# Log-sum-exp over rows: splitting the rows 111 and 17 per partition instead of 112 and 16

## Chip, cores and metric

The kernel runs on one core of one Trainium2 chip. The metric is device time in microseconds, the median of several executions. Lower is better.

## What is computed

The input `x` has shape 32 x 512 x 1024 in float32 (64 MB). For each of its 16,384 rows of 1024 values the kernel returns the logarithm of the sum of exponentials:

```python
def reference(x):
    max_x = np.max(x, axis=-1, keepdims=True)
    return (max_x.squeeze(-1) + np.log(np.sum(np.exp(x - max_x), axis=-1))).astype(np.float32)
```

The inputs are drawn from a normal distribution, so the kernel sums plain exponentials without subtracting the maximum, checks that no sum is out of bounds, and only if one is repeats everything with the maximum taken off.

## The kernel before

There are 128 rows for each of the 128 partitions. They come from two regions of the input. In the first, partition p holds `W = 112` rows that follow one another in memory; in the second it holds `B = 16` rows that do so (`x_rows` and `x_rest`, lines 81 and 82). The output is written in the same two regions, with one store each (`out_rows`, line 329, and `out_rest`, line 343).

The rows travel through a ring in SBUF with room for 48 rows per partition. SyncE issues all loads on one queue, in order (line 157). Before each load it waits until the reductions that read that part of the ring are over; `users` keeps the list.

The first region comes in the nine loads of `LOADS`, each with its size in rows and with what is done to it. ScalarE takes the exponential of each group in place (line 236). A group marked R is then summed by VectorE over all 1024 columns (line 251). A group marked F is first folded by GpSimd, which adds the second half of each row to the first (line 244); VectorE then sums 512 columns per row (line 199, in `reduce_folded`). `F2+2` means two folds of two rows each.

The second region comes in nine "late" loads, whose sizes get smaller. The order is: from column `HEAD` = 528 of the region to `start`; from row `MID` to 608 columns (`BACK`) before the end; the five `PIECES`, which fill the space from `start` to row `MID`; the last 608 columns; the first 528 columns. `start` is `MID * d - sum(PIECES)`, with `d` = 1024. ScalarE takes the exponential of each piece (line 294). As soon as a row of the region is complete, VectorE sums it by adding its two halves with an accumulator (`halves`, line 208). Rows cut by `HEAD` and `BACK` are summed in parts, and the parts of the first pass are joined to the last two pieces as logarithms (line 322), so that the last two exponentials (lines 287 and 279) sum them on ScalarE.

In the middle of this ScalarE takes the logarithm of the first region's sums (line 314), and VectorE checks the columns that are ready (`check_early`, lines 166 and 171). TensorE adds up the later checks in one PSUM cell (line 186). At the end come a last check on VectorE (lines 334 and 351), the last logarithms on ScalarE (lines 339 and 341), the second store, and the test of the check (line 358), on which the branch depends.

The order on each engine is the order of the code, and each engine waits on semaphores that the others count up.

Of the kernel before, what the change touches and what calls it, by code (L numbers as in the profile page):

```python
# [13 lines left out]
CEILING = 27.0  # L14
STEEP = 2.0**48
RING = 48
B = 16
GAP = 32
AHEAD = 1
FIRST = 512  # L20
# [1 line left out]

LOADS = [
    (16, "R16"), (16, "R16"), (16, "R16"), (16, "F9 R7"), (13.5, "F6 R7"), (12.5, "R7 F6"),
    (9, "R5 F4"), (7, "F4 R3"), (6, "F2+2 R2"),
]

HEAD, BACK, MID = 528, 608, 12  # L30
PIECES = [2656, 2000, 1456, 1088, 800]


# [23 lines left out]
def kernel(  # L57
# [21 lines left out]
    H = d // 2  # L79
    W = NC - B  # L80
    x_rows = x_flat[0 : P * W].rearrange("(p c) d -> p (c d)", p=P)
# [15 lines left out]
    start = MID * d - sum(PIECES)  # L97
    late = [(HEAD, start), (MID * d, B * d - BACK)]
    for size in PIECES:
        late.append((start, start + size))  # L100
        start += size
    late += [(B * d - BACK, B * d), (0, HEAD)]
    assert start == MID * d and sum(e - s for s, e in late) == B * d
    LATE = W + late[0][1] // d
# [114 lines left out]
    for i, (size, ops) in enumerate(loads):  # L219
# [37 lines left out]
        assert here == end  # L257
    assert c == W and here == p and p + GAP + B * d <= RING * d

    gap = p + (B - MID) * d  # L260

# [212 lines left out]
```

## Time and profile before

| | |
|---|---|
| median of 3 runs | 161.6 us (161.47 to 161.63) |
| the profiled execution | 161.53 us |
| its span, first to last instruction | 160.2 us |
| granted clock | 1.000 |
| VectorE busy | 114.2 us (71% of the span) |
| ScalarE busy | 114.5 us (71%) |
| GpSimd busy | 37.3 us (23%) |
| load queue's share of the 16 DMA engines | 97.9% |
| read from HBM | 67.11 MB |

Times in the profile count from the first instruction of the span. "ACT" is ScalarE, "DVE" is VectorE, "POOL" is GpSimd, "SP" is SyncE and "SPq" its queue, where DMAs are issued. A line of the timeline gives start, duration, engine, line and operation, and in brackets how long the engine was idle before and what ended it. In the groups by line and shape, the number behind the bar is the busy time in us, then the mean of one in ns, then the idle time before. A DMA issue is shown with its size and the time from issue to landing.

### The profile page before, as it was taken

The numbers are of one execution on the slowest core, as the hardware profiler recorded it, in microseconds if no ns is written. First come the engines' busy times: TensorE is split into PE (matmuls) and PEld (weight loads), VectorE is DVE, ScalarE is ACT, GpSimd is POOL, SyncE is SP. The second block draws the span as 40 slices with busy tenths as digits, with TensorE's granted clock in tenths as the row PEclk, the third lists the DMA queues.
The fourth block names the chain that finished last, engine by engine and source line by source line (L and its number), as shares of the span: only waits on it lengthen the run. The fifth ranks groups of instructions, "written<-read, shape, count | busy, mean of one in ns | idle before, by whom it ended". The sixth has DMA issues, their size and how long they took to land.

```text
span 160.2 us, 236 instructions
## 1 busy us (share of the span) xinstructions
PE 2.3 (1%) x32; PEld 1.2 (1%) x32; DVE 114.2 (71%) x60; ACT 114.5 (71%) x31; POOL 37.3 (23%) x11
## 2 busy tenths in 40 slices
PE   0000000000000000000000000000000000000023
PEld 0000000000000000000000000000000000000011
DVE  0000000019999499994999859959999999999996
ACT  3000059980799709995099949992999989799996
POOL 0000000000000000000000994690004969765000
DMA  9996996996996996996999999999989999999993
GB/s 319 507 491 269 507 524 262 524 524 262 524 524 262 524 507 278 524 491 295 483 442 442 442 425 409 409 409 481 414 387 445 458 409 393 425 433 425 414 405 111
DMA packets 3025, 67.18 MB, mean 419 GB/s; under 512 B 592, under 2 KB 592, under 8 KB 1488
## 3 DMA queue, kind: packets, MB, share of 16 engines
q1 hardware_dynamic: 3024, 67.18, 97.9%
q14 instruction: 1, 0.01, 0.0%
HBM read 67.11 MB, written 0.07 MB: 419 GB/s over the span
## 4 chain that ended last, share of the span: by engine, by line
DMA 51%; ACT 27%; DVE 20%; issue 0%; PE 0%
DMA ring<-in_x_dram 51%; ACT ring L236 19%; DVE sumexp L251 16%; ACT ring L294 7%; DVE sumexp L199 2%; DVE ring L208 2%; DVE over L351 0%; PE count L356 0%; ACT res L314 0%; DVE clamped L334 0%; DVE fine L358 0%; ACT ring L322 0%
## 5 line engine op out<-in xcount | busy, mean ns | idle before, releaser
L236 ACT ACTIVATE ring<-ring 128x16384 f32<-128x16384 f32 (+9 forms) x15 | 97.9, 6568 | 42.3 <-DMA ring<-in_x_dram 42.3
L251 DVE TENSOR_REDUCE sumexp<-ring 128x16 f32<-128x16384 f32 (+4 forms) x9 | 85.6, 9515 | 42.4 <-ACT ring L236 42.4
L244 POOL TENSOR_TENSOR ring<-ring 128x3072 f32<-128x3072 f32 (+3 forms) x7 | 37.1, 5313 | 108.8 <-ACT ring L236 108.8
L199 DVE TENSOR_REDUCE sumexp<-ring 128x6 f32<-128x3072 f32 (+3 forms) x7 | 18.4, 2657 | 0.0
L294 ACT ACTIVATE ring<-ring 128x3760 f32<-128x3760 f32 (+6 forms) x7 | 13.9, 2009 | 0.0
L208 DVE SCALAR_TENSOR_TENSOR ring<-ring 128x512 f32<-128x512 f32 (+2 forms) x16 | 9.5, 650 | 0.1
L142 ACT ACT_TABLE_LOAD x1 | 1.3, 1283 | 1.9 <-PEq L66 1.9
L176 PE MATMUL count<-far,bad 128*1 128x1 f32 x2 | 0.2, 164 | 152.9 <-DVE clamped L171 152.9
L186 PE MATMUL count<-sumexp,ones 128*1 128x1 f32 x24 | 1.9, 164 | 3.5 <-DVE ring L208 3.5
L143 DVE MEMSET ones<- 128x1 f32 x1 | 0.1, 59 | 2.0 <-PEq L66 2.0
L208 DVE DVE_READ_ACCUMULATOR ring<-ring 128x1 f32 x16 | 1.3, 82 | 0.0
L176 PEld LDWEIGHTS count<-far,bad 128*1 128x1 f32 x2 | 0.1, 80 | 152.9 <-DVE clamped L171 152.9
L186 PEld LDWEIGHTS count<-sumexp,ones 128*1 128x1 f32 x24 | 0.9, 81 | 4.4 <-DVE ring L208 4.4
L287 ACT ACTIVATE ring<-ring 128x610 f32<-128x610 f32 x1 | 0.7, 696 | 0.0
L279 ACT ACTIVATE last_exp<-ring 128x530 f32<-128x530 f32 x1 | 0.6, 595 | 0.0
L351 DVE SCALAR_TENSOR_TENSOR over<-ring 128x264 f32<-128x264 f32 x1 | 0.4, 427 | 0.0
L358 DVE TENSOR_SCALAR fine<-count 1x1 int32<-1x1 f32 x1 | 0.1, 146 | 0.3 <-PE count L356 0.3
L171 DVE SCALAR_TENSOR_TENSOR clamped<-clamped,sumexp 128x117 f32<-128x117 f32 x1 | 0.3, 281 | 0.0
L314 ACT ACTIVATE res<-sumexp 128x112 f32<-128x112 f32 x1 | 0.3, 280 | 0.0
L166 DVE TENSOR_SCALAR clamped<-sumexp 128x117 f32<-128x117 f32 x1 | 0.2, 224 | 0.0
L339 ACT ACTIVATE res<-sumexp 128x15 f32<-128x15 f32 x1 | 0.2, 203 | 0.0
L334 DVE SCALAR_TENSOR_TENSOR clamped<-sumexp 128x12 f32<-128x12 f32 x1 | 0.2, 170 | 0.0
(20 smaller groups left out, 2.3 us busy)
## 6 DMA issues: line engine op xcount, KB each, us to landing
ring<-in_x_dram SPq DMA_DIRECT2D x1, 7936.0 KB, 21.3
ring<-in_x_dram SPq DMA_DIRECT2D x1, 6912.0 KB, 23.9
ring<-in_x_dram SPq DMA_DIRECT2D x1, 6400.0 KB, 19.7
ring<-in_x_dram SPq DMA_DIRECT2D x1, 4608.0 KB, 15.9
ring<-in_x_dram SPq DMA_DIRECT2D x1, 3584.0 KB, 24.0
ring<-in_x_dram SPq DMA_DIRECT2D x1, 3072.0 KB, 19.1
ring<-in_x_dram SPq DMA_DIRECT2D x1, 1880.0 KB, 16.0
ring<-in_x_dram SPq DMA_DIRECT2D x1, 1744.0 KB, 19.8
```

The lines of the kernel that those rows point to most:

```text
L142: nc.scalar.preload_act_table_set("natural_log_exp_and_others")
L176: pe.did(nc.tensor.matmul(count, lhsT=bad[:, 0:1], rhs=far, start=True, stop=False))
L186: pe.did(nc.tensor.matmul(count, lhsT=ones, rhs=sumexp[:, c : c + 1], start=False, stop=False))
L199: at = dve.did(nc.vector.reduce_sum(out=sumexp[:, c0 : c0 + s0], in_=halves, axis=AX.X))
L208: return dve.did(nc.vector.scalar_tensor_tensor(out=v[:, 0:n], in0=v[:, 0:n], scalar=1.0, in1=v[:, n : 2 * n], op0=ALU.mult, op1=ALU.add, ...
L236: at = act.did(nc.scalar.activation(out=v, in_=v, func=AF.Exp))
L244: at = pool.did(nc.gpsimd.tensor_tensor(out=lo, in0=lo, in1=rows[:, r : r + m, H:d], op=ALU.add))
L251: at = dve.did(nc.vector.reduce_sum(out=sumexp[:, c : c + s], in_=rows, axis=AX.X))
L279: head_sum = act.did(nc.scalar.activation(out=last_exp[:, 0 : e - s + 2], in_=ring[:, at0 - 2 : at1], func=AF.Exp, accum_out=last_sum,))
L287: back_sum = act.did(nc.scalar.activation(out=v, in_=v, func=AF.Exp, accum_out=sumexp[:, NC - 1 : NC]))
L294: at = act.did(nc.scalar.activation(out=v, in_=v, func=AF.Exp))
L351: dve.did(nc.vector.scalar_tensor_tensor(out=over, in0=ring[:, at0 : at0 + half], scalar=CEILING, in1=ring[:, at0 + half : at1], op0=ALU.m ...
```

## The change

The second region gets 17 rows per partition instead of 16, and so the first region 111 instead of 112. The ninth load has 5 rows instead of 6, of which 3 instead of 4 are folded (two and one). `MID` moves from 12 to 13, so that the five pieces and the other three late loads keep their sizes. The first late load goes from column 528 to column 5312 of the region and has 4784 columns instead of 3760; one more of the region's rows is complete with it. The rows of one partition lie 111 rows (444 KB) and 17 rows (68 KB) behind those of the partition before it in memory, instead of 448 and 64 KB. The two stores write 444 and 68 bytes per partition instead of 448 and 64.

```diff
-B = 16
+B = 17
...
 LOADS = [
     (16, "R16"), (16, "R16"), (16, "R16"), (16, "F9 R7"), (13.5, "F6 R7"), (12.5, "R7 F6"),
-    (9, "R5 F4"), (7, "F4 R3"), (6, "F2+2 R2"),
+    (9, "R5 F4"), (7, "F4 R3"), (5, "F2+1 R2"),
 ]
...
-HEAD, BACK, MID = 528, 608, 12
+HEAD, BACK, MID = 528, 608, 13
 PIECES = [2656, 2000, 1456, 1088, 800]
```

## The prediction

> **What bounds the kernel now.** I read the page first, then the chain of waits in order of time, the DMA issues, and last the timeline of the final 45 us engine by engine.
>
> ```profile
> span 160.2 us, 236 instructions
> q1 hardware_dynamic: 3024, 67.18, 97.9%
> DMA 51%; ACT 27%; DVE 20%; issue 0%; PE 0%
> ```
>
> The load queue is busy for 97.9% of the 16 DMA engines' time. The chain gives DMA only 51%, because it follows one releaser at each step. So the load stream sets the pace, and the question is what happens behind its last pieces.
>
> ```profile
> 118.89 19.10 DMA ring<-in_x_dram
> 138.01 5.42 ACT ring L236 x2
> 143.43 6.32 ACT ring L294 x2
> ...
> 154.20 1.31 ACT ring L294
> 155.54 2.55 DVE ring L208 x8
> ```
>
> The chain leaves DMA at 138.0, when the ninth load (six rows) lands. From there it runs over ScalarE's exponentials, and over four row sums on VectorE at the end. Whether ScalarE is really the limit is told by the landings, which come from the issue times (SPq rows) and the times to landing:
>
> ```profile
> 126.42 0.33 SPq L157 DMA_DIRECT2D ring<-in_x_dram  x1
> 126.79 1.38 SPq L157 DMA_DIRECT2D ring<-in_x_dram  x3
> ring<-in_x_dram SPq DMA_DIRECT2D x1, 1880.0 KB, 16.0
> ring<-in_x_dram SPq DMA_DIRECT2D x1, 1744.0 KB, 19.8
> ring<-in_x_dram SPq DMA_DIRECT2D x1, 1000.0 KB, 24.5
> 138.01 5.42 ACT L236 ACTIVATE ring<-ring 128x4096 f32<-128x4096 f32 x2 [1.03 <-DMA ring<-in_x_dram]
> 143.33 6.41 ACT L294 ACTIVATE ring<-ring 128x3760 f32<-128x3760 f32 x2
> 146.64 3.11 ACT L294 ACTIVATE ring<-ring 128x3488 f32<-128x3488 f32 x1
> 149.84 4.27 ACT L294 ACTIVATE ring<-ring 128x2656 f32<-128x2656 f32 x2
> L294 ACT ACTIVATE ring<-ring 128x2000 f32<-128x2000 f32 x1 | 1.9, 1870 | 0.0
> ```
>
> The first late load (1880 KB) is issued at 126.42 and lands 16.0 later, at 142.4. ScalarE takes it at 143.33, 0.9 us late, because it is still busy with the ninth load. The second (1744 KB) lands at 126.79 + 19.8 = 146.6, and ScalarE takes it at 146.64, that is, at its landing. The fourth (1000 KB) is the third of the three issues from 126.79; with about 0.45 us between issues it goes out near 127.7 and lands at 152.2. The last row's two exponentials end at 149.84 + 4.27 = 154.11, so the second (2000 columns, 1.87 us) starts at 152.2, again at its landing. After that ScalarE has no gap up to the last store. So the end is the landing of the fourth late load plus a fixed piece of ScalarE's work. What lies before 152.2 counts only if it moves a landing, or makes ScalarE miss one.
>
> **The change part by part.** The loads. The ninth load falls from 6 to 5 rows and the first late one grows from 3760 to 4784 columns, which is the same 1024. The two lie next to each other in the queue, so the first late load and all that follow land where they did. The number of transfers is unchanged. The ninth load itself lands earlier by 1024 columns:
>
> ```profile
> 41.09 13.86 ACT L236 ACTIVATE ring<-ring 128x16384 f32<-128x16384 f32 x1 [5.49 <-DMA ring<-in_x_dram]
> 60.45 13.86 ACT L236 ACTIVATE ring<-ring 128x16384 f32<-128x16384 f32 x1 [5.50 <-DMA ring<-in_x_dram]
> ```
>
> Two loads of 16 rows are 19.36 us apart, so a row takes 1.21 us and the ninth load lands at 138.0 - 1.2 = 136.8. SP's waits are the same: the ninth load overwrites rows that the same reduction frees, the first late load waits for the same two reductions, and the later pieces fall on the same places of the ring, because the start moves down a row and the piece offset moves up one. The late load is issued at 126.4 and the queue is occupied with the ninth until 136.8, so 10 us of cover are left for that issue.
>
> ScalarE, with these rows:
>
> ```profile
> 130.71 6.27 ACT L236 ACTIVATE ring<-ring 128x4096 f32<-128x4096 f32 x2 [0.54 <-DMA ring<-in_x_dram]
> L236 ACT ACTIVATE ring<-ring 128x4096 f32<-128x4096 f32 x3 | 10.8, 3612 | 1.6 <-DMA ring<-in_x_dram 1.6
> L236 ACT ACTIVATE ring<-ring 128x5120 f32<-128x5120 f32 x1 | 4.5, 4471 | 0.0
> L236 ACT ACTIVATE ring<-ring 128x3072 f32<-128x3072 f32 x1 | 2.7, 2748 | 0.0
> L236 ACT ACTIVATE ring<-ring 128x2048 f32<-128x2048 f32 x1 | 1.9, 1893 | 0.0
> ```
>
> The eighth load's exponentials end at 130.71 + 6.27 = 136.98, so the ninth load now finds ScalarE busy for 0.2 us instead of idle for 1.03. Its two exponentials have 3072 and 2048 columns, 2.75 + 1.89 less an overlap of 0.09 (3.61 + 1.89 against the 5.42 in the timeline), so they end at 136.9 + 4.55 = 141.5. ScalarE then waits for the landing at 142.4. The exponential of 4784 columns costs, between the rows of 4096 and 5120 (0.84 ns a column), 3612 + 688 x 0.84 = 4190 ns, and the next can start 4.10 after it: 142.45 + 4.10 = 146.55. The second late load lands at 146.6. The longer piece just fits, with 0.05 to 0.1 to spare, where before it started 0.9 late and was 0.85 shorter. Another 0.1 is lost harmlessly between 149.84 and the landing at 152.2. ScalarE's term is 0.
>
> VectorE and GpSimd:
>
> ```profile
> 140.82 2.28 DVE L199 TENSOR_REDUCE sumexp<-ring 128x4 f32<-128x2048 f32 x1
> 143.46 2.29 DVE L251 TENSOR_REDUCE sumexp<-ring 128x2 f32<-128x2048 f32 x1 [0.37 <-ACT ring L236]
> 145.66 2.34 DVE L199 TENSOR_REDUCE sumexp<-ring 128x2 f32<-128x1024 f32 x2
> 147.92 0.68 DVE L208 SCALAR_TENSOR_TENSOR ring<-ring 128x512 f32<-128x512 f32 x1
> 154.14 0.69 DVE L208 SCALAR_TENSOR_TENSOR ring<-ring 128x512 f32<-128x512 f32 x1
> 155.54 0.69 DVE L208 SCALAR_TENSOR_TENSOR ring<-ring 128x512 f32<-128x512 f32 x1
> L199 DVE TENSOR_REDUCE sumexp<-ring 128x4 f32<-128x2048 f32 x2 | 4.6, 2276 | 0.0
> L199 DVE TENSOR_REDUCE sumexp<-ring 128x2 f32<-128x1024 f32 x2 | 2.3, 1210 | 0.0
> L208 DVE SCALAR_TENSOR_TENSOR ring<-ring 128x512 f32<-128x512 f32 x14 | 8.9, 687 | 0.1
> L244 POOL TENSOR_TENSOR ring<-ring 128x1024 f32<-128x1024 f32 x2 | 4.7, 2359 | 2.4 <-ACT ring L236 2.4
> ```
>
> One folded row leaves the ninth load. The second folded reduction shrinks from 1024 to 512 columns; by the two L199 rows that is 1210 - 533 = 0.68 us, 0.53 saved. GpSimd's second addition halves to some 1.2 us, and its pair, starting at 139.7, ends at 143.3, well before VectorE asks for it. One more row sum (L208) comes with the first late load: 0.61 us, the pitch at which they follow each other (0.69 with its tail overlapped). The reduction of the last two rows no longer waits 0.37 for ScalarE: it starts at 143.1 when VectorE is free. So the row sums can start at 143.1 + 2.2 + 1.1 + 0.7 = 147.1 or 147.2 instead of 147.92, and after five instead of four VectorE stands 0.1 earlier than before. That is worth nothing, because at 154.14 and 155.54 VectorE waits for exponentials that end at 154.11 and 155.51, and the last four sums follow the second of these as before. If the savings failed, the extra 0.61 would meet a slack of about 0.11 at 154.14 and 0.17 at 155.54 (each start less the end of the row sum before it, at a pitch of 0.61). VectorE's term is 0.
>
> The stores. The logarithms and checks change by one column; their term is 0. Each partition's result piece becomes 444 and 68 bytes instead of 448 and 64.
>
> ```profile
> 158.76 0.34 SPq L343 DMA_DIRECT2D out_dram<-res  x1
> out_dram<-res SPq DMA_DIRECT2D x1, 56.0 KB, 1.6
> out_dram<-res SPq DMA_DIRECT2D x1, 8.0 KB, 1.4
> ```
>
> The last store goes out at 158.76 and lands 1.4 later, at 160.2, which is the span: its length counts in full. The first (56 KB) lands at about 158.8 and stays hidden. The trace has no store whose pieces cross a multiple of 64 bytes, as nearly every 68-byte one does. Bounds: nothing (half a KB more, between rows that differ by 48 KB and 0.2 us), and +0.4 if each such write took a second round, which I put at a bit under a third of the 1.4. I take +0.05, near the row of its own size.
>
> The source pitch. A partition's rows lie 444 and 68 KB apart in memory instead of 448 and 64. The trace shows no difference between those two old pitches: 16 rows in 19.36 us is 433 GB/s, and the first late load, the first at 64 KB, took 142.4 - 138.0 = 4.4 us for 1.925 MB, 437 GB/s by rounded times. I take 0. The only stretch that is slower is the start:
>
> ```profile
> 0.00:1.00 1.00, 0.00 (x0) 0.00 (x0) 0.00 (x0) 0.00 (x0) 0.20 (x4) 1.00 0.00 0
> 21.74 13.86 ACT L236 ACTIVATE ring<-ring 128x16384 f32<-128x16384 f32 x1 [18.54 <-DMA ring<-in_x_dram]
> ```
>
> The first 16 rows land at 21.7, which is 2.4 more than 19.36, and 1.0 of that passes before any byte moves. The other 1.4 holds the first round of the transfers, which no pitch removes, and whatever the 128 row starts do to each other. So the bounds on the pitch are 1.4 either way at the start.
>
> The sum: loads 0, ScalarE 0, VectorE 0, store +0.05, pitch 0. The profiled execution took 161.53, of which 160.2 is the span and 1.3 lies around it. It would become 161.58, and the median of three, 161.6, becomes 161.65. A measurement of this kernel can tell about 0.2%, 0.32 us, from no change.
>
> **The rivals.** First, slower: the last store pays for pieces off the 64-byte grid. For it: nothing follows that could hide it. Against: no row shows such a cost, and 7 times the bytes cost only 0.2. It is dearer than the bound when issue to landing passes 1.7; at a second round of 0.4 the time is 162.0. The Trainium skill ("DMA: Bandwidth & Descriptors", "How a descriptor splits into AXI transactions") says that reads are cut at multiples of 256 bytes, with an extra transaction where a piece starts off them; if writes went likewise, about a quarter of the 68-byte pieces would split, and none of the 64-byte ones did. No run here shows its price.
>
> Second, faster: the row starts, 448 KB apart, collide at the start, and 444 spreads them. For it: the 1.4 us. Against: nothing slows later, at either pitch. A third of the 1.4 is 0.5, so 161.15; the same thing the other way, 162.15. The Trainium skill (same page, "Latency and other measured facts") reports copies slowed by row pitches of large powers of two, from 512 KiB up, and cured by 4 KiB more; by that rule the move from 64 to 68 KB would help the late loads. Its table begins far above 64 KB, and the trace does not agree that 64 KB is slow (437 GB/s beside 433).
>
> Third, slower: VectorE becomes the bound. If its 0.53 and its earlier start fail to appear, the extra row sum's 0.61 less the slack of 0.28 gives +0.33, 162.0. Against: the three rows above.
>
> **How the numbers follow.** Forecast 0.46; store 0.20; pitch faster 0.18, pitch slower 0.08; VectorE 0.08. So faster 0.18, same 0.46, slower 0.36. The forecast's own range is 161.3 to 161.95. The whole range reaches down to the pitch at 161.15 and up to the pitch at 162.15; beyond lie the larger shares of the 1.4 and a dearer store, under 2 in 10.
>
> **What would show it.** Right: the ninth load's exponential starts near 136.9; the first late one at 142.45 with 4.19; ScalarE idles 0.9 before it; the second late one starts at 146.6; VectorE's row sums start near 147.2; the last store lands 1.4 to 1.5 after its issue. Wrong: a first load that lands away from 21.7; a last store over 1.7; a second late exponential after 146.75; last row sums with no wait at 155.5.

## The result: 0.4% slower, by a transfer that the change does not name

The changed kernel takes 162.25 us (162.09 to 162.47), the kernel before 161.62 (161.47 to 161.71), both with 6 runs. The ratio is 1.0041, with an interval of 1.0028 to 1.0054, or +0.63 us. The forecast was 161.65, with 161.15 to 162.15 around it. The profiled execution of the changed kernel took 162.34.

The page of the changed kernel, span and chain:

```profile
span 161.0 us, 237 instructions
DMA 50%; ACT 27%; DVE 17%; another core or an unknown queue 3%; SPq 1%; issue 0%; PE 0%; DVEq 0%
```

The span grew by 0.8. The chain by engine says little. In order of time it says more: it now leaves DMA at 157.92, where it left it at 138.0 before.

```profile
137.10 20.82 DMA ring<-in_x_dram
157.94 0.81 ACT ring L287 x2
```

Here is the timeline of ScalarE and VectorE at the places that the prediction named:

```profile
22.05 13.86 ACT L236 ACTIVATE ring<-ring 128x16384 f32<-128x16384 f32 x1 [18.85 <-DMA ring<-in_x_dram]
142.76 7.28 ACT L294 ACTIVATE ring<-ring 128x4784 f32<-128x4784 f32 x2 [1.03 <-DMA ring<-in_x_dram]
147.23 0.68 DVE L208 SCALAR_TENSOR_TENSOR ring<-ring 128x512 f32<-128x512 f32 x1
154.42 0.69 DVE L208 SCALAR_TENSOR_TENSOR ring<-ring 128x512 f32<-128x512 f32 x1 [0.33 <-ACT ring L294]
157.94 0.71 ACT L287 ACTIVATE ring<-ring 128x610 f32<-128x610 f32 x1 [0.39 <-DMA ring<-in_x_dram]
```

Two things are new. The first load lands at 22.05 instead of 21.74, and everything behind it is 0.3 later (142.76 where 142.45 was expected). And ScalarE waits 0.39 for the load of the last 608 columns: its exponential starts at 157.94, and not 0.3 but 0.75 later than in the kernel before, where ScalarE did not wait:

```profile
157.19 0.70 ACT L287 ACTIVATE ring<-ring 128x610 f32<-128x610 f32 x1
```

The second step is in the times to landing of the last two loads, first of the kernel before, then of the changed one:

```profile
ring<-in_x_dram SPq DMA_DIRECT2D x1, 304.0 KB, 20.3
ring<-in_x_dram SPq DMA_DIRECT2D x1, 264.0 KB, 20.5
```

```profile
ring<-in_x_dram SPq DMA_DIRECT2D x1, 304.0 KB, 20.8
ring<-in_x_dram SPq DMA_DIRECT2D x1, 264.0 KB, 21.0
out_dram<-res SPq DMA_DIRECT2D x1, 8.5 KB, 1.4
```

Both loads take 0.5 longer. The last store takes 1.4, as before. What else ran on the DMA engines there is in the table of queues, which has a line "q14 instruction" with one transfer of 8 KB. Asked of narrow windows, it lies at 158.4 to 159.0 in the kernel before and at 156.3 to 156.7 in the changed one:

```profile
q14 instruction: 1, 0.01, 5.1%
```

In the trace's packet records it starts at 158.49 in the kernel before, after the last load has landed and before the last store moves a byte. In the changed kernel it starts at 156.36, among the last two loads. In the records of these loads four packets there take 175 to 295 ns instead of 86 or 98. VectorE's program is the likely cause: line 331 asks that VectorE's end part start on a multiple of 128 instructions, and before the change VectorE's queue has a branch there, over the padding, which is gone in the changed kernel:

```profile
L331 DVEq COMPARE_BRANCH  x1: 51/51/51, 157.3 to 157.3; - x1
```

The extra row sum is two instructions (the sum and the reading of its accumulator), and two seemed to be what the padding had held. So there were two suspects, the fetch and the late first load, and the source pitch of 111 rows was the only part of the change that touches the first load.

### The profile page after: what moved, and what is told of

Its sections match the earlier page's. It is cut to its first block, busy times and chain, and to the rows that moved or that the text cites. A ratio compares the mean times of both kernels' runs of the same rounds, so it can differ in the third digit from the quotient of the medians.

```text
span 161.0 us, 237 instructions
## 1 busy us (share of the span) xinstructions
PE 2.5 (2%) x32; PEld 1.2 (1%) x32; DVE 114.2 (71%) x62; ACT 114.6 (71%) x31; POOL 36.2 (22%) x11
## 4 chain that ended last, share of the span: by engine, by line
DMA 50%; ACT 27%; DVE 17%; another core or an unknown queue 3%; SPq 1%; issue 0%; PE 0%; DVEq 0%
DMA ring<-in_x_dram 50%; ACT ring L236 27%; DVE sumexp L251 14%; DVE sumexp L199 2%; SPq L157 1%; ACT ring L287 1%; DVE over L351 0%; PE count L356 0%; DVE clamped L334 0%; DVE fine L358 0%; DVEq L53 0%
## 5 line engine op out<-in xcount | busy, mean ns | idle before, releaser
L244 POOL TENSOR_TENSOR ring<-ring 128x3072 f32<-128x3072 f32 (+4 forms) x7 | 36.0, 5157 | 107.1 <-ACT ring L236 107.1
L199 DVE TENSOR_REDUCE sumexp<-ring 128x6 f32<-128x3072 f32 (+4 forms) x7 | 17.9, 2580 | 0.0
L294 ACT ACTIVATE ring<-ring 128x4784 f32<-128x4784 f32 (+6 forms) x7 | 14.7, 2132 | 1.0 <-DMA ring<-in_x_dram 1.0
L208 DVE SCALAR_TENSOR_TENSOR ring<-ring 128x512 f32<-128x512 f32 (+2 forms) x17 | 10.2, 651 | 0.4 <-ACT ring L294 0.3
```

Of the source, the lines that this page charges most:

```text
L199: at = dve.did(nc.vector.reduce_sum(out=sumexp[:, c0 : c0 + s0], in_=halves, axis=AX.X))
L208: return dve.did(nc.vector.scalar_tensor_tensor(out=v[:, 0:n], in0=v[:, 0:n], scalar=1.0, in1=v[:, n : 2 * n], op0=ALU.mult, op1=ALU.add, ...
L244: at = pool.did(nc.gpsimd.tensor_tensor(out=lo, in0=lo, in1=rows[:, r : r + m, H:d], op=ALU.add))
L294: at = act.did(nc.scalar.activation(out=v, in_=v, func=AF.Exp))
```

## Experiments

All times below are medians. The kernel before took 161.54 to 161.61 beside them.

**1. VectorE's program as long as before, in the changed kernel.**

```diff
-    dve.did(nc.vector.memset(steep, STEEP))
-    less_at = dve.did(nc.vector.memset(less, ...))
+    pool.did(nc.gpsimd.memset(steep, STEEP))
+    less_at = pool.did(nc.gpsimd.memset(less, ...))
+    pe.wait(pool, less_at)
...
-    pe.wait(dve, less_at)
+    pe.wait(pool, less_at)
```

> The changed kernel with two of VectorE's four constant fills moved to GpSimd, so that VectorE's program ahead of its end part is again as many instructions long as before the change. Theory A (two causes: an 8 KB instruction fetch that moved from 158.5 to 156.4, into the last loads, costs about 0.4; a first load that lands 0.3 late because of the 111-row pitch costs the rest): the fetch goes back behind the loads, the load of 608 columns lands near 157.4 instead of 157.9, the first load still lands near 22.0, and the time is 161.8 to 161.95. Theory B (the late first load is all there is, and the fetch only happens to lie there): 162.25, unchanged. Theory C (fetch alone; the late first load is chance): 161.6.

Measured: 161.92, ratio 1.0022 (1.0013 to 1.0031). The branch is back, here on line 332, and the fetch starts at 158.95.

```profile
L332 DVEq COMPARE_BRANCH  x1: 51/51/51, 157.8 to 157.8; - x1
22.22 13.86 ACT L237 ACTIVATE ring<-ring 128x16384 f32<-128x16384 f32 x1 [19.02 <-DMA ring<-in_x_dram]
157.63 0.70 ACT L288 ACTIVATE ring<-ring 128x610 f32<-128x610 f32 x1
```

ScalarE no longer waits for the 608 columns, although the first load was later still in this execution. Moving the fetch back gave 0.33. Theory B falls, and so does C, since 0.34 stays.

**2. Two more instructions in the kernel before**, as fills of an unused tile at the start.

```diff
+    spare = sbuf("spare", 2)
+    dve.did(nc.vector.memset(spare[:, 0:1], 1.0))
+    dve.did(nc.vector.memset(spare[:, 1:2], 1.0))
     less_at = dve.did(nc.vector.memset(less, ...))
```

> The kernel before with two more constant fills on VectorE at its start, into a tile that nobody reads, which makes its program as long as that of the changed kernel; rows, loads and pitch as before. Theory A: the fetch appears near 156.3, the load of 608 columns lands about 0.4 to 0.5 late (157.5 to 157.6 instead of 157.1), the first load lands at 21.7, and the time is 161.9 to 162.1. Theory B: 161.6, no difference. Theory C: 162.2.

> The kernel before with two more fills on VectorE once more, for a second profile: the first load was 0.34 late in the first one although its pitch is 448 KB. If that was chance of one execution: first load at 21.7 here, one of the last two loads late, 161.9 to 162.2. If it belongs to this kernel: 22.05 again.

Measured: 162.13, ratio 1.0036 (1.0024 to 1.0048), and 162.13 again, ratio 1.0032 (1.0021 to 1.0043). The fetch starts at 156.61 and 156.50. Two instructions that compute nothing, at the start of a kernel of 161.6 us, cost 0.5 us at its end. In the first profile the first load was 0.34 late, in the second 0.12 (ScalarE starts on it at 21.86); so a part of the first reading was chance of one execution, and one late first load in a profile doesn't prove an effect of the pitch; the medians of experiments 1 and 3 do that. In the first profile ScalarE waits for the load of 528 columns, in the second for that of 608. The second is the cleaner one, though it is the slowest of its 7 runs (162.44):

```profile
158.03 0.71 ACT L290 ACTIVATE ring<-ring 128x610 f32<-128x610 f32 x1 [0.64 <-DMA ring<-in_x_dram]
```

**3. The pitch of 111 alone, in the kernel before.**

```diff
-    x_rows = x_flat[0 : P * W].rearrange("(p c) d -> p (c d)", p=P)
+    x_rows = bass.AP(tensor=x_flat.tensor, offset=x_flat.offset, ap=[[111 * d, P], [1, W * d]])
```

> The kernel before, but each partition's 112 rows of the first region are read from 111 rows behind those of the partition before it, so that neighbours share a row; the second region is as before. This changes the source addresses alone (the results of the first region are then not the reference's). Theory A: the first load lands near 22.0 instead of 21.7, the fetch stays at 158.5, the time is 161.8 to 161.95. Theory B: 162.2. Theory C: 161.6 with the first load at 21.7 or scattered around it.

Measured: 161.96, ratio 1.0024 (1.0015 to 1.0033); fetch at 158.72, behind the loads.

```profile
21.98 13.86 ACT L236 ACTIVATE ring<-ring 128x16384 f32<-128x16384 f32 x1 [18.77 <-DMA ring<-in_x_dram]
41.33 13.86 ACT L236 ACTIVATE ring<-ring 128x16384 f32<-128x16384 f32 x1 [5.49 <-DMA ring<-in_x_dram]
```

The first load is 0.24 late, and the second comes 19.35 behind it, as before (19.36). The loss is made once and kept.

**4. Both taken back in the changed kernel** (the edits of 1 and 3, with 112 in place of 111).

> The changed kernel with both taken back: the two fills on GpSimd, and the first region's 111 rows read 112 rows apart (results of that region not the reference's). The cut of loads and late pieces, the extra row sum, the 68-byte store and the 68 KB pitch of the second region stay. Theories A, B and C all expect 161.6 here; a time above 161.8 says that the cut, the store or the second region's pitch costs something of its own.

Measured: 161.57, ratio 1.0000 (0.9991 to 1.0009).

```profile
21.75 13.86 ACT L237 ACTIVATE ring<-ring 128x16384 f32<-128x16384 f32 x1 [18.55 <-DMA ring<-in_x_dram]
157.17 0.70 ACT L288 ACTIVATE ring<-ring 128x610 f32<-128x610 f32 x1
```

So the new cut of the loads, the extra row sum, the 68-byte store and the second region's pitch of 68 KB cost nothing that these runs can tell.

**5. The fetch alone, in the changed kernel** (the pitch of 112, VectorE's program as changed).

> The changed kernel with its first region's 111 rows read 112 rows apart, nothing else taken back (results of that region not the reference's): the early fetch alone, in the changed kernel. If the two causes add: 162.25 less the 0.34 that the pitch cost with the fetch behind the loads (161.92 against 161.58), so 161.9, with the fetch near 156.1 and a first load at 21.7. If the fetch only costs much when one engine is late already: under 161.75.

Measured: 162.24, ratio 1.0035 (1.0021 to 1.0049). I had expected 161.9, and that was wrong: the two do not add.

```profile
21.81 13.86 ACT L236 ACTIVATE ring<-ring 128x16384 f32<-128x16384 f32 x1 [18.60 <-DMA ring<-in_x_dram]
157.83 0.71 ACT L287 ACTIVATE ring<-ring 128x610 f32<-128x610 f32 x1 [0.52 <-DMA ring<-in_x_dram]
```

With a first load in time, the 608 columns still come at 157.83, against 157.94 with both. The fetch alone is +0.63, the pitch alone +0.34, both together +0.63. The trace's records of landings show why. Each load's semaphore rises in 16 steps, as many as there are DMA engines, and ScalarE goes on after the last of them (157.92 for the 608 columns of the changed kernel, where ScalarE starts at 157.94). The last two steps of the last load lie at 157.75 and 157.78 in the kernel before, at 157.82 and 158.47 here, and at 158.06 and 158.56 in the changed kernel. So with both causes two steps are late, one by each, and the later one counts: the fetch hit another engine than the one that lagged from the start. No record names the engines.

**6. The branch without an added instruction, and an added instruction without its effect on the branch.** First the alignment asked for two instructions earlier, then two fills behind the aligned part.

```diff
-    nc.vector.addr_align(128, offset=0, max_nops=0)
+    nc.vector.addr_align(128, offset=126, max_nops=0)
```

> The kernel before with the alignment of VectorE's end part asked for two instructions earlier, where its program stands by itself, so that no branch is put in front of it. No instruction is added; rows, loads and pitch as before. Theory A (the branch holds the fetch back; without it the fetch falls into the last loads): the fetch moves to 156.4 to 157.4, the first load lands at 21.7 as before, one of the last two loads lands late, and the time is 161.8 to 162.0 (0.2 to 0.4 of the 0.55 of the kernel with two more fills, whose first load was 0.34 late in its profile too). Theory D (the length of VectorE's program, not the fetch, costs the time): 161.6.

> The kernel before with two more fills on VectorE behind the aligned part, ahead of its wait for TensorE's last product: VectorE's program is as long as the changed one's, but all that lies before the alignment is as before. Theory A: fetch at 158.5, first load at 21.7, 161.6 to 161.65. Theory D: the first load lands 0.3 late and the time is 161.9.

Measured: the first 162.05, ratio 1.0026 (1.0017 to 1.0035), the second 161.50, ratio 0.9997 (0.9988 to 1.0006), with its fetch at 158.50. The length of the program by itself is therefore free. The first has no branch and is slower, but not as I had thought: its fetch came later, at 159.19, and hit the last store: 15 of that store's 16 steps come by 160.35, the last at 160.68.

```profile
158.52 0.08 DVE L334 DVE_READ_ACCUMULATOR clamped<-sumexp 128x1 f32 x1 [0.26 <-issue]
158.93 0.34 SPq L343 DMA_DIRECT2D out_dram<-res  x1
out_dram<-res SPq DMA_DIRECT2D x1, 8.0 KB, 1.7
```

VectorE stood still for 0.26 in its end part, for nothing that the profile shows, the store went out 0.17 later (158.93 against 158.76), and it took 1.7 instead of 1.4. Why VectorE stood still isn't shown: the fetch starts only after that. Between the last load and the last store there is a gap in which the fetch is free; the kernel before has it there.

**7. One fill and three.**

> The kernel before with one more fill on VectorE instead of two. If the early fetch comes of the missing branch, and two instructions fill the gap exactly: the branch is still there at 157.3, the fetch at 158.5, 161.6. If each instruction ahead of the end part moves the fetch: between 156.4 and 158.5, 161.8 to 162.1.

> The kernel before with three more fills on VectorE. If two fill the gap, three overrun it: a branch appears again, since the end part now goes to the next boundary, but the program crosses the first boundary before that branch, so that there is a fetch near 156 and the time is 162.0 or more, with a second fetch later. If the branch alone decides: the fetch 1.2 us behind the branch, 161.6.

Measured: one fill 161.58, ratio 1.0001 (0.9991 to 1.0010), branch at 157.35 and fetch at 158.54. Three fills 162.33, ratio 1.0051 (1.0034 to 1.0068), with a branch again, and two fetches, at 156.27 and 158.85:

```profile
L335 DVEq COMPARE_BRANCH  x1: 51/51/51, 157.3 to 157.3; - x1
q14 instruction: 2, 0.02, 1.8%
157.92 0.71 ACT L291 ACTIVATE ring<-ring 128x610 f32<-128x610 f32 x1 [0.66 <-DMA ring<-in_x_dram]
```

So two instructions fill the gap exactly, and it is not a shift of the fetch by a little with each. While a branch leads across the boundary, the fetch comes about 1.2 us behind it (157.33 and 158.49 before the change; 1.5 with three fills, where it is the second fetch). Where the part of VectorE's program ahead of its end part runs up to the boundary or over it, a fetch comes at 156.1 to 156.6, whether a branch follows (three fills) or not (the changed kernel).

**8. Other pitches of the first region, and 111 in the first load only**, in the kernel before.

```diff
+    x_near = bass.AP(tensor=x_flat.tensor, offset=x_flat.offset, ap=[[111 * d, P], [1, W * d]])
...
     def source(e0, size):
+        if e0 + size <= 16 * d:
+            return x_near[:, e0 : e0 + size]
```

> The kernel before with its first region's 112 rows read 113 rows apart (one row of each 113 is left out; results not the reference's). Theory P1 (a pitch of a multiple of 16 rows, 64 KB, starts the 16 engines well, others badly): first load 0.2 to 0.5 late, 161.85 to 162.0. Theory P2 (111 is a bad number by itself): 161.6.

> The kernel before with its first region's 112 rows read 128 rows (512 KB) apart, so that 16 rows of each 128 are left out (results not the reference's). Theory P1: 161.6, as 128 is a multiple of 16. Theory P3 (large powers of two collide): the first load later than 22, and more than 162.0, or a lower rate in every load.

> The kernel before with only the first 16 of the 112 rows of each partition read 111 rows apart; the other loads keep 112 (results of the first 16 rows are not the reference's). If the pitch costs its time in the first load alone, by the engine that falls behind there and never catches up: first load at 22.0 to 22.2, all later landings late by the same, 161.85 to 162.0, as with 111 throughout (161.96). If every load pays a little: 161.65 or less.

Measured: 113 rows 161.58, ratio 1.0006 (0.9997 to 1.0015); 128 rows 162.25, ratio 1.0040 (1.0026 to 1.0053); 111 in the first load only 161.84, ratio 1.0016 (1.0007 to 1.0025). The start of the first exponential in each, and of the second for 128:

```profile
21.79 13.86 ACT L236 ACTIVATE ring<-ring 128x16384 f32<-128x16384 f32 x1 [18.59 <-DMA ring<-in_x_dram]
```

```profile
22.49 13.86 ACT L236 ACTIVATE ring<-ring 128x16384 f32<-128x16384 f32 x1 [19.28 <-DMA ring<-in_x_dram]
41.82 13.86 ACT L236 ACTIVATE ring<-ring 128x16384 f32<-128x16384 f32 x1 [5.48 <-DMA ring<-in_x_dram]
```

```profile
21.93 13.86 ACT L239 ACTIVATE ring<-ring 128x16384 f32<-128x16384 f32 x1 [18.73 <-DMA ring<-in_x_dram]
```

That multiples of 64 KB start well (P1) is refuted twice: 113 is as good as 112, and 128 is worse than 111. The first load carries 0.23 of the 0.35 or so that 111 costs throughout, with intervals that overlap. Of the four pitches 512 KB was the worst, but at the start only: with 128 rows the second load comes 19.33 behind the first. It also looks different in the landings: with 128 rows most of the first load's 16 steps are late (21.66 to 22.46, against 21.35 to 21.72 before the change), with 111 only one to three (in experiment 1 one at 22.20, the others by 21.71). The Trainium skill ("DMA: Bandwidth & Descriptors", "Latency and other measured facts") reports copies slightly slowed at 512 KiB; here that pitch costs 0.7 us once and no rate afterwards. What makes 111 worse than 112 and 113 stays open; only four pitches were tried.

## Why the prediction was wrong, point by point

The step that failed is the first term of the sum, "Loads 0". It said that the first late load and all that follow land where they did, since bytes and transfers are the same. But the addresses of the first region had changed, and a transfer of another queue had moved among the last loads. Landings moved by 0.31 from the first load on, and by 0.8 at the last two.

The larger part was missed altogether. I costed the extra row sum as 0.61 us of VectorE's time, which was right and hidden, and not as two instructions in a program whose length is aligned by hand at line 331. The page had the transfer in its table of queues, "q14 instruction", and the trace had the branch at 157.3. I gave neither a price, and made no rival of them. The runs showed +0.63 for it in the changed kernel and +0.5 in the kernel before.

"Pitch 0" failed too, as a term that measured +0.34 by itself. The rival that the pitch would act at the start was right in its place, but I gave the faster side 0.18 and the slower one 0.08, and it was the slower one. In the final time it is hidden under the fetch. That its 162.15 lies near the measured 162.25 is luck: the time came from the fetch, which no rival had. Two of the signs of being wrong came true, the late first load and a second late exponential after 146.75, and both told of the pitch alone.

Right were the terms inside the engines. ScalarE waited 1.03 before the first late load (0.9 foretold), took 4.19 for it as foretold, and ran 142.76 + 7.28 without a gap over the second; its start, 3.11 before that end, is 146.93, which is 146.6 and the 0.31 by which all was late. VectorE's row sums started at 147.23 (147.2 foretold), though everything else was late, and it then waited 0.33 for ScalarE at 154.42, so that it did not become the bound. The last store took 1.4 with pieces of 68 bytes, so the store rival, at 0.20 the likeliest, was wrong, and its +0.05 measured nothing. (One reading there was loose: the 448-byte pieces of the first store do cross multiples of 64 bytes; what the trace lacked were pieces that start off them.)

The Trainium skill ("Runtime: NRT & Kernel Launch", "Instruction fetch mechanics") would have put the fetch at nothing: it says that crossing into the next block of instructions is mostly hidden, and that a taken branch to a place outside the blocks at hand is what causes a stall. Here the crossing cost 0.5 to 0.6 us through the loads beside it, and with the branch it stayed harmless; the measurement decides.

## What to carry to other kernels

An edit can change the length of an engine's program, and with it the moment of the next instruction fetch. So count added instructions as well as their time, look for "instruction" in the table of DMA queues and for alignment calls in the code, and see which load or store the fetch will meet. Where loads bound a kernel, a transfer of 8 KB on one engine can count, because a load is as late as its latest engine; two such delays on different engines did not add here, the later one counted.

## What the runs showed of the hardware

- One instruction fetch of 8 KB (0.33 us in the records of the changed kernel) held up the last two loads by 0.5 us there and by 0.6 in experiment 5, more than its own length: in experiment 5 three packets of 2432 bytes took 284, 335 and 335 ns where 98 is the rule. In each of the five profiles with an early fetch (the changed kernel, experiment 5, two fills twice, three fills) such lengthened packets took 0.66 to 0.70 us more than usual in all.
- A fetch at 159.19 made the last store 0.3 us longer (1.7 against 1.4, one profile).
- Why the fetch comes near 156.3 when the program runs up to the boundary, 1.3 us before the last row sum ahead of the boundary starts (156.36 and 157.67 in the changed kernel), is not shown by these runs; reading ahead would explain it, but the fetch at 159.19 in experiment 6 doesn't fit a fixed distance.
- The pitch between partitions' rows changed when the first load lands, but not the rate afterwards. ScalarE starts on that load at 21.7 to 21.9 with 448 KB (22.1 in one profile of nine), at 21.8 with 452, which is no difference, at 21.9 to 22.2 with 444 and at 22.5 with 512 (one profile each for 452 and 512, four for 444).
